# Modulation sums by transposes, narrower attention levels, and a low-rank column with its halves side by side: one decoder layer

## Chip, cores and metric

The kernel runs on one core of a Trainium2 chip. The metric is the device time of one execution in microseconds (us), the median of several runs. The core's engines run their own instruction queues in order: TensorE (PE, matrix multiplications and transposes, with its weight loads, PEld, beside them), VectorE (DVE), ScalarE (ACT), GpSimd (POOL) and SyncE (SP), from whose queue nearly all transfers (DMA) are issued.

## What is computed

One layer of a hybrid decoder, 256 tokens of width 2048, all in float32:

```python
mod = silu(c) @ w_ada + b_ada                      # six segments of 2048
shift1, scale1, gate1, shift2, scale2, gate2 = split(mod, 6)
h = rms_norm(x, norm1_gain) * (1 + scale1) + shift1
proj = h @ w_in                                    # 2048 x 13840, split into
#   stick-breaking q, k, v; dilated q, k, v; GLA q, k, v, r;
#   a_gla (16 columns, the low-rank forget gate); 3 x 2048 branch gates
a = a_gla @ w_gla_a + b_gla_a                      # 16 -> 512
log_a = log_sigmoid(a) / 16
o_gla = rms_norm(gla(q, k, v, log_a)) * silu(r)    # gated linear attention
y = g0 * (o_sb @ w_br_sb) + g1 * (o_dil @ w_br_dil) + g2 * (o_gla @ w_br_gla)
x = x + gate1 * (y @ w_out)
h = rms_norm(x, norm2_gain) * (1 + scale2) + shift2
x = x + gate2 * ((silu(gate) * up) @ w_ffn_out)    # gate, up = h @ w_ffn_in
```

In the gated linear attention the score of query i and key j (j not after i) is the sum over the channels of q_i k_j exp(cum_i - cum_j), where cum is the running sum of log_a over the tokens.

## The kernel before

**Matrix products.** Activations are kept transposed in 128-row chunks, split into a high part rounded to a reduced 32-bit matmul type (float32r) and a low part with the rest. Weights get the same split: `load_weights` (line 124) brings 1024 columns a partition (2 chunks of 512, or 8 chunks of 128) by one DMA into a buffer `raw`, ACT rounds it into `whi` (147), DVE subtracts into `wlo` (148). `raw`, `whi` and `wlo` are rings of four buffers each. `mm3` (lines 152 to 155) then makes three matmuls for each pair: high x high, high activation x low weight, low activation x high weight. `block` (157) runs them for one block of 512 output columns and both halves of the tokens into the four `acc` banks of PSUM; four further banks, `misc`, serve everything else. A matmul of plain float32 operands is also used (attention, sums, the low-rank gate).

**Modulation.** `ada_mac` (258) multiplies a row block of `w_ada` by one column of silu(c) and adds it to an accumulator `ada` on DVE, so that after 16 chunks the accumulator's sum over the 128 partitions is the wanted row. `column_sum` (301) makes that sum and turns the row into a column at once: the 128 x 128 piece of the accumulator is the stationary operand and a column of ones the moving one. `finish_columns` (303) adds the bias (307) and, for a scale, adds 1 and multiplies by the norm's gain (310). For the first norm the 16 chunks come in four groups (`GROUPS`, 3, 4, 4 and 5 chunks); `first_group` has its own code, `ada_group` (264) does the others in pieces of 4, 4, 2 and 3 chunks while `proj_block` already multiplies the preceding group with `w_in`. `h_group` then makes that group's part of h. For the second norm `columns` (798) does the same for 16 chunks of shift2 and of scale2 as a background generator, advanced by `tick` between matmuls; its result is used by `norm2` (line 1016).

**Mixing.** While the last group of chunks runs over the 13 blocks of `w_in`, `stick_breaking`, `gla` and `dilated` are placed among the matmuls. `gla` (618) first multiplies h with 128 columns of `w_in` that begin with the 16 of the low-rank gate: it loads them with `load_weights` and runs 16 x `mm3` with the weight stationary and 256 tokens moving, then copies 16 rows to `aT` and multiplies these with `w_gla_a`. The scores within a tile of 128 tokens are built by levels: for L = 1, 2, 4, ... 64, keys in the even runs of L tokens meet queries in the following odd run. Factors exp(...) for both sides lie in one tile `f`; `scatter` (674) multiplies the whole 128 x 128 tile for the 4 heads (678) and copies those entries that the level's 0/1 mask selects (679). Entries of level L have a key below 128 - L and a query from L on.

**Order.** The program's order is a proposal: a planner places the instructions on each engine by priorities (`prio` raises them) and by the buffers that are free; `issue_after` sets an instruction behind another one on its engine. Once placed, each engine's order is fixed.

Of the kernel before, what the change touches and what calls it, by code (L numbers as in the profile page):

```python
# [10 lines left out]
F32 = mybir.dt.float32  # L11
F32R = mybir.dt.float32r
# [25 lines left out]
GROUPS = ((0, 3), (3, 7), (7, 11), (11, 16))  # L38
GLA_LEVELS = (1, 2, 4, 8, 16, 32, 64)
NFF = 11  # L40
ROW_N1, ROW_N2, ROW_SBQ, ROW_SBK, ROW_DILQ, ROW_DILK, ROW_GB, ROW_GG = 16, 32, 48, 49, 50, 51, 52, 56


# [22 lines left out]
def trunk(ctx: ExitStack, tc: tile.TileContext, I, out):  # L66
# [11 lines left out]
    def nm(base):  # L78
        uid[0] += 1
        return f"{base}_{uid[0]}"  # L80

    def S(tag, shape, dtype=F32):
        return slot.tile(shape, dtype, tag=tag, name=nm(tag))

    def small(shape, dtype=F32, bufs=8):
        return sp.tile(shape, dtype, tag="tiny", name=nm("tiny"), bufs=bufs)

    def scr(shape, dtype=F32):
        return sp.tile(shape, dtype, tag="scr", name=nm("scr"))
# [4 lines left out]
    def misc_bank(shape):  # L94
        return psm.tile(shape, F32, tag="misc", name=nm("misc"))
# [28 lines left out]
    def load_weights(src, k0, k1, c0, w=NB, spare=(), ahead=True):  # L124

        parts = []
        step = (2 * NB) // w  # L130
        with prio() if ahead else nullcontext():
            for ka in range(k0, k1, step):
                n = min(step, k1 - ka)
                raw = wp.tile([P, step, w], F32, tag="raw", name=nm("raw"))
                nc.sync.dma_start(
                    raw[:, :n, :],
                    src[ka * P : (ka + n) * P, c0 : c0 + w].rearrange("(k p) c -> p k c", p=P),
                )
                i = len(spare) - (k1 - ka)
                if i >= 0:  # L140
                    hi = S(spare[i], [P, step, w], F32R)
                    lo = S(spare[i + 1], [P, step, w], F32R)
                else:
                    hi = wp.tile([P, step, w], F32R, tag="whi", name=nm("whi"), bufs=4)
                    lo = wp.tile([P, step, w], F32R, tag="wlo", name=nm("wlo"), bufs=4)
                with tc.issue_after(state["casts_after"]) if "casts_after" in state else nullcontext():
                    state["cast"] = nc.scalar.copy(hi[:, :n, :], raw[:, :n, :])  # L147
                state["split"] = nc.vector.tensor_tensor(lo[:, :n, :], raw[:, :n, :], hi[:, :n, :].bitcast(F32), op=ALU.subtract)  # L148
                parts += [(hi[:, i, :], lo[:, i, :]) for i in range(n)]
        return parts  # L150

    def mm3(ps, lh, ll, rh, rl, start, stop, seeded=False):
        nc.tensor.matmul(ps, lh, rh, start=start, stop=False, skip_group_check=seeded)  # L153
        nc.tensor.matmul(ps, lh, rl, start=False, stop=False, skip_group_check=seeded)  # L154
        state["mm"] = nc.tensor.matmul(ps, ll, rh, start=False, stop=stop, skip_group_check=seeded)  # L155
# [108 lines left out]
    def ada_group(k0, k1, tags=ADA_TAGS, between=None):  # L264

        n = k1 - k0
        sh, sc = mod1[:, 0, k0:k1], mod1[:, 1, k0:k1]
        count = 0
        pieces = -(-n // 4)
        for i in range(pieces):  # L270
            a = k0 + n * i // pieces
            m = k0 + n * (i + 1) // pieces - a
            w = m * P
            acc = S("ada", [P, 2, w])
            for k in range(KC):
                with prio():
                    raw = S(tags[count % len(tags)], [P, 2, w])
                    nc.sync.dma_start(
                        raw,
                        w_ada[k * P : (k + 1) * P, : 2 * D].rearrange("p (s c) -> p s c", s=2)[:, :, a * P : a * P + w],  # L280
                    )
                    ada_mac(acc, raw, k)
                count += 1
                if k < KC - 1:
                    yield
            if between is not None:
                between()
            with prio():
                o = a - k0
                for q in range(m):  # L290
                    ps = misc_bank([P, 2])
                    for j in range(2):
                        column_sum(ps[:, j : j + 1], acc[:, j, q * P : (q + 1) * P])
                    c = slice(o + q, o + q + 1)
                    finish_columns(ps[:, 0:1], sh[:, c], SEG_SHIFT1, a + q)
                    finish_columns(ps[:, 1:2], sc[:, c], SEG_SCALE1, a + q, ROW_N1)
            yield
        gains[GROUPS.index((k0, k1))] = (sh, sc)

    def column_sum(ps, acc):  # L300
        return nc.tensor.matmul(ps, acc, ones[:, 0:1], start=True, stop=True)  # L301

    def finish_columns(ps, dst, seg, k0, gain_row=None):

        n = dst.shape[1]
        o = seg * KC + k0
        nc.vector.tensor_tensor(dst, ps, bada[:, o : o + n], op=ALU.add)
        if gain_row is not None:
            g = vec[:, gain_row + k0 : gain_row + k0 + n]
            nc.vector.scalar_tensor_tensor(dst, dst, 1.0, g, op0=ALU.add, op1=ALU.mult)  # L310
# [229 lines left out]
    lvl_f = S("T4", [P, len(GLA_LEVELS) + 1, P])  # L540
    nc.sync.dma_start(lvl_f, I["k_lvl"])
    nc.gpsimd.tensor_copy(lvl, lvl_f)
    wga = kc[:16, 4:8, :].rearrange("p a b -> p (a b)")
    nc.sync.dma_start(wga, I["w_gla_a"])

    def head(c, t):
        return A[c // 4][:, t, (c % 4) * P : (c % 4 + 1) * P]
# [68 lines left out]


    def gla():
        aw = load_weights(w_in, 0, KC, COL_A, P)
        ps = misc_bank([P, T])  # L620
        for k in range(KC):
            hh = hT[0][k // 4][:, k % 4, :]
            hl = hT[1][k // 4][:, k % 4, :]
            mm3(ps, aw[k][0], aw[k][1], hh, hl, k == 0, k == KC - 1)
        aT = scr([16, T])
        nc.scalar.copy(aT, ps[:16, :])

        for b in (9, 10, 11, 12):
            proj_block(LAST, b)
# [41 lines left out]
        def at(x, h, t):  # L671
            return x[:, h * T + t * P : h * T + (t + 1) * P]

        def scatter(level, lhs, rhs):
            for t in range(NT):
                ps = misc_bank([P, N_GLA, P])
                for h in range(N_GLA):
                    nc.tensor.matmul(ps[:, h, :], at(lhs, h, t), at(rhs, h, t), start=True, stop=True)  # L678
                nc.vector.copy_predicated(
                    sc_same[t], lvl[:, level : level + 1, :].to_broadcast([P, N_GLA, P]), ps  # L680
                )

        scatter(len(GLA_LEVELS), kT, qT)
        for li, L in enumerate(GLA_LEVELS + (P,)):
            f = S(f"T{4 + li % 2}", [P, N_GLA * T])
            view = lambda x: x.rearrange("p (s two l) -> p s two l", two=2, l=L)
            fv, pw, sw, qw, kw = view(f), view(pre), view(suf), view(qT), view(kT)
            nc.scalar.activation(fv[:, :, 0, :], sw[:, :, 0, :], AF.Exp, scale=1.0 / 16.0)
            nc.scalar.activation(fv[:, :, 1, :], pw[:, :, 1, :], AF.Exp, scale=1.0 / 16.0)
            nc.vector.tensor_mul(fv[:, :, 0, :], fv[:, :, 0, :], kw[:, :, 0, :])  # L690
            nc.vector.tensor_mul(fv[:, :, 1, :], fv[:, :, 1, :], qw[:, :, 1, :])
            if L < P:
                scatter(li, f, f)
                ns = N_GLA * T // (2 * L)
                nc.vector.tensor_tensor(
                    sw[:, :, 0, :], sw[:, :, 0, :], pw[:, :, 1, L - 1 : L].to_broadcast([P, ns, L]), op=ALU.add
                )
                nc.vector.tensor_tensor(
                    pw[:, :, 1, :], pw[:, :, 1, :], pw[:, :, 0, L - 1 : L].to_broadcast([P, ns, L]), op=ALU.add
                )  # L700
            else:
                ps = misc_bank([P, N_GLA, P])
                for h in range(N_GLA):
                    nc.tensor.matmul(ps[:, h, :], at(f, h, 0), at(f, h, 1), start=True, stop=True)
                nc.scalar.copy(sc_cross, ps)
# [92 lines left out]
    def columns(seg, acc):  # L798
        for _ in range(4):
            yield  # L800
        v = const.tile([P, KC], F32, name=nm("mod2"))
        for i in range(0, KC, 4):
            ps = misc_bank([P, 4])
            for j in range(4):
                with tc.issue_after(state["mm"].ins):
                    column_sum(ps[:, j : j + 1], acc[:, (i + j) * P : (i + j + 1) * P])
                if j % 2:
                    yield
            finish_columns(ps, v[:, i : i + 4], seg, i, ROW_N2 if seg == SEG_SCALE2 else None)
        mod2[seg] = v  # L810

    def rows_of(name, seg, acc):
# [344 lines left out]
```

## Time and profile before

| what | us |
|---|---|
| median of 3 runs | 1636.75 (1636.34 to 1638.01) |
| profiled execution | 1638.33 |
| its span | 1636.6 |
| casts on ACT (line 147, 1024 wide), busy | 549.4 |
| subtractions on DVE (line 148, 1024 wide), busy | 636.6 |
| low-rank column on PE, first to last start | 338.5 to 344.2 |
| levels on PE, first to last start | 364.4 to 401.3 |
| core's granted TensorE clock | 1.00 |

A row of a group in this profile reads: line, engine, operation, output <- inputs with their shapes, count | busy us, mean ns of one | idle time of the engine just before them, and what ended it. A row of the timeline begins with the start and the duration. A row of the waits gives who waited for whom, then us in total, times, and the longest. Matmuls of one engine overlap: the next begins before the last one's result is written, so a mean duration is longer than the distance from start to start.

### The profile page before, as it was taken

The page shows a single profiled execution, that of the slowest core. Times are in us where ns is not written, and L with a number is a line of the kernel's source. Part 1 is how long each engine was busy: PE and PEld are TensorE (multiplying, and loading weights), DVE is VectorE, ACT ScalarE, POOL GpSimd, SP SyncE. Part 2 cuts the span into 40 slices and gives each one's busy share as a digit, 9 for nine tenths or more (in the row PEclk, how much of TensorE's full clock was granted, in tenths as well). Part 3 has the DMA queues.
Part 4 walks back from the last instruction along what each step waited for, and adds up shares of the span by engine and source line. Part 5 has one row for each costly group of instructions (what it writes and reads, how often), then busy time and mean ns, then how long its engine had stood idle before and what let it go on. Part 6 is the DMA issues. An engine that isn't in the chain of part 4 may idle for free.

```text
span 1636.6 us, 20156 instructions
## 1 busy us (share of the span) xinstructions
PE 1617.2 (99%) x7420; PEld 1333.7 (81%) x7420; DVE 1120.2 (68%) x1342; ACT 798.2 (49%) x1126; POOL 5.9 (0%) x14
## 2 busy tenths in 40 slices
PE   8999999999999999999999999999999999999998
PEld 7888888778778888788887888888888888888887
DVE  6789996879688687877756566767655555454453
ACT  5654449764765444444445644444444444433332
POOL 1000000000000000000000000000000000000000
PEclk9999999999999999999999999999999999999999
DMA  9999986876778889888756478887766666666663
GB/s 318 340 324 320 331 283 209 257 229 186 224 233 276 289 303 320 294 272 310 260 185 222 133 229 268 274 262 257 220 187 191 182 191 189 190 206 193 206 206 110
DMA packets 194563, 395.93 MB, mean 242 GB/s; under 512 B 12899, under 2 KB 27913, under 8 KB 194465
## 3 DMA queue, kind: packets, MB, share of 16 engines
q1 hardware_dynamic: 194240, 394.63, 74.3%
q8 instruction: 58, 0.95, 0.2%
q14 instruction: 41, 0.33, 0.1%
q0 software_dynamic: 224, 0.01, 0.0%
HBM read 392.50 MB, written 2.10 MB: 241 GB/s over the span
## 4 chain that ended last, share of the span: by engine, by line
PE 90%; DMA 4%; DVE 3%; ACT 2%; issue 1%; SPq 0%; DVEq 0%; ACTq 0%
PE acc L154 28%; PE acc L155 28%; PE acc L153 28%; DMA raw<-w_in 2%; DVE wlo L148 1%; DMA A<-w_ada 1%; PE misc L678 1%; ACT whi L147 1%; PE misc L943 1%; PE misc L301 1%; DVE ada L258 1%; DMA raw<-w_br_gla 0%; PE misc L572 0%; DMA AR<-w_ada 0%; DMA raw<-w_ffn_in 0%
## 5 line engine op out<-in xcount | busy, mean ns | idle before, releaser
L148 DVE TENSOR_TENSOR wlo<-raw,whi 128x1024 fp32r<-128x1024 f32 (+1 forms) x548 | 653.6, 1197 | 436.4 <-ACT whi L147 432.9
L147 ACT CAST whi<-raw 128x1024 fp32r<-128x1024 f32 (+1 forms) x548 | 564.7, 1033 | 720.0 <-PE acc L155 559.0
L154 PE MATMUL acc<-wlo,H 128*128 128x512 f32 x1576 | 617.0, 391 | 4.8 <-DVE wlo L148 4.5
L155 PE MATMUL acc<-whi,H 128*128 128x512 f32 x1576 | 615.3, 391 | 0.0
L153 PE MATMUL acc<-whi,H 128*128 128x512 f32 x1576 | 614.6, 392 | 0.6 <-ACT H L408 0.5
L154 PEld LDWEIGHTS acc<-wlo,H 128*128 128x128 f32 x1576 | 296.0, 188 | 68.9 <-DVE wlo L148 9.5
L155 PEld LDWEIGHTS acc<-whi,H 128*128 128x128 f32 x1576 | 295.9, 188 | 61.8 <-DVE H L1021 0.9
L153 PEld LDWEIGHTS acc<-whi,H 128*128 128x128 f32 x1576 | 295.6, 188 | 61.5 <-ACT H L408 0.9
L153 PE MATMUL acc<-whi,A 128*128 128x512 f32 x312 | 122.4, 392 | 0.0
L154 PE MATMUL acc<-wlo,A 128*128 128x512 f32 x312 | 121.5, 390 | 0.8 <-DVE wlo L148 0.8
L155 PE MATMUL acc<-whi,A 128*128 128x512 f32 x280 | 109.1, 390 | 0.0
L258 DVE SCALAR_TENSOR_TENSOR ada<-AR,csil,ada 128x1024 f32<-128x1024 f32 x59 | 75.1, 1279 | 3.2 <-DMA AR<-w_ada 3.1
L154 PEld LDWEIGHTS acc<-wlo,A 128*128 128x128 f32 x312 | 58.6, 188 | 12.9 <-DVE wlo L148 1.1
L153 PEld LDWEIGHTS acc<-whi,A 128*128 128x128 f32 x312 | 58.6, 188 | 12.2 <-ACT whi L147 0.3
L155 PEld LDWEIGHTS acc<-whi,A 128*128 128x128 f32 x280 | 52.5, 188 | 11.1
L153 PE MATMUL acc<-whi,T 128*128 128x512 f32 x120 | 46.8, 390 | 0.0
L155 PE MATMUL acc<-whi,T 128*128 128x512 f32 x120 | 46.7, 389 | 0.0
L154 PE MATMUL acc<-wlo,T 128*128 128x512 f32 x120 | 46.7, 389 | 0.0
L155 PE MATMUL acc<-whi,OS 128*128 128x512 f32 x112 | 43.6, 389 | 0.0
L258 DVE SCALAR_TENSOR_TENSOR ada<-OS,csil,ada 128x1024 f32<-128x1024 f32 (+2 forms) x33 | 35.5, 1075 | 0.8 <-DMA OS<-w_ada 0.5
L453 DVE TENSOR_TENSOR A<-A,acc 128x512 f32<-128x512 f32 x48 | 31.9, 684 | 5.1 <-PE acc L155 4.9
L451 ACT COPY A<-acc 128x512 f32<-128x512 f32 x50 | 28.4, 585 | 11.8 <-PE acc L155 10.8
(327 smaller groups left out, 1246.1 us busy)
## 6 DMA issues: line engine op xcount, KB each, us to landing
raw<-w_in SPq DMA_DIRECT2D x205, 512.0 KB, 4.8
raw<-w_ffn_in SPq DMA_DIRECT2D x176, 512.0 KB, 3.8
raw<-w_ffn_out SPq DMA_DIRECT2D x88, 512.0 KB, 4.7
AR<-w_ada SPq DMA_DIRECT2D x79, 512.0 KB, 4.7
raw<-w_out SPq DMA_DIRECT2D x32, 512.0 KB, 3.9
KC<-w_ada SPq DMA_DIRECT2D x30, 512.0 KB, 5.2
KD<-w_ada SPq DMA_DIRECT2D x19, 512.0 KB, 5.5
OS<-w_ada SPq DMA_DIRECT2D x16, 512.0 KB, 7.3
```

The source lines that it names most:

```text
L147: state["cast"] = nc.scalar.copy(hi[:, :n, :], raw[:, :n, :])
L148: state["split"] = nc.vector.tensor_tensor(lo[:, :n, :], raw[:, :n, :], hi[:, :n, :].bitcast(F32), op=ALU.subtract)
L153: nc.tensor.matmul(ps, lh, rh, start=start, stop=False, skip_group_check=seeded)
L154: nc.tensor.matmul(ps, lh, rl, start=False, stop=False, skip_group_check=seeded)
L155: state["mm"] = nc.tensor.matmul(ps, ll, rh, start=False, stop=stop, skip_group_check=seeded)
L258: nc.vector.scalar_tensor_tensor(acc, raw, c, acc, op0=ALU.mult, op1=ALU.add)
L301: return nc.tensor.matmul(ps, acc, ones[:, 0:1], start=True, stop=True)
L451: nc.scalar.copy(A[b][:, t, :], pss[t])
L453: nc.vector.tensor_add(A[b][:, t, :], A[b][:, t, :], pss[t])
L678: nc.tensor.matmul(ps[:, h, :], at(lhs, h, t), at(rhs, h, t), start=True, stop=True)
L943: nc.tensor.transpose(ps[:, i, :], src[:, i * P : (i + 1) * P], ident)
```

## The change

Four edits. The sum over partitions is made by transposing the 128 x 128 pieces (up to four into one bank) and adding along the rows on DVE; in `columns` the bias and gain are applied once at the end, on all 16 columns. `scatter` gets the level's L and uses keys 0 to 127 - L and queries L to 127 alone. The 16 low-rank columns are split into a tile `T6` of their own, high and low side by side as 32 stationary columns: one matmul with the high part of h gives both products (rows 0 to 15 and 16 to 31), a second one adds the low part of h times the high weights to rows 0 to 15. `w_gla_a` is loaded twice, below itself, so that the product with the 32 rows adds the halves. `first_group` and `rows_of` stay as they are.

```diff
--- before.py
+++ after.py
@@ -38,6 +38,7 @@
 GROUPS = ((0, 3), (3, 7), (7, 11), (11, 16))
 GLA_LEVELS = (1, 2, 4, 8, 16, 32, 64)
 NFF = 11
+RANK = 16
 ROW_N1, ROW_N2, ROW_SBQ, ROW_SBK, ROW_DILQ, ROW_DILK, ROW_GB, ROW_GG = 16, 32, 48, 49, 50, 51, 52, 56
 
 
@@ -286,19 +287,26 @@
             if between is not None:
                 between()
             with prio():
-                o = a - k0
-                for q in range(m):
-                    ps = misc_bank([P, 2])
-                    for j in range(2):
-                        column_sum(ps[:, j : j + 1], acc[:, j, q * P : (q + 1) * P])
-                    c = slice(o + q, o + q + 1)
-                    finish_columns(ps[:, 0:1], sh[:, c], SEG_SHIFT1, a + q)
-                    finish_columns(ps[:, 1:2], sc[:, c], SEG_SCALE1, a + q, ROW_N1)
+                c = slice(a - k0, a - k0 + m)
+                sums = small([P, 2, m])
+                for j in range(2):
+                    turned_sums(sums[:, j, :], acc[:, j, :])
+                finish_columns(sums[:, 0, :], sh[:, c], SEG_SHIFT1, a)
+                finish_columns(sums[:, 1, :], sc[:, c], SEG_SCALE1, a, ROW_N1)
             yield
         gains[GROUPS.index((k0, k1))] = (sh, sc)
 
     def column_sum(ps, acc):
         return nc.tensor.matmul(ps, acc, ones[:, 0:1], start=True, stop=True)
+
+    def turned_sums(dst, acc, behind=None):
+
+        n = dst.shape[1]
+        ps = misc_bank([P, n, P])
+        for i in range(n):
+            with tc.issue_after(behind) if behind is not None else nullcontext():
+                nc.tensor.transpose(ps[:, i, :], acc[:, i * P : (i + 1) * P], ident)
+        nc.vector.reduce_sum(dst, ps, axis=AX.X)
 
     def finish_columns(ps, dst, seg, k0, gain_row=None):
 
@@ -540,8 +548,9 @@
     lvl_f = S("T4", [P, len(GLA_LEVELS) + 1, P])
     nc.sync.dma_start(lvl_f, I["k_lvl"])
     nc.gpsimd.tensor_copy(lvl, lvl_f)
-    wga = kc[:16, 4:8, :].rearrange("p a b -> p (a b)")
-    nc.sync.dma_start(wga, I["w_gla_a"])
+    wga = kc[: 2 * RANK, 4:8, :].rearrange("p a b -> p (a b)")
+    for i in range(2):
+        nc.sync.dma_start(wga[i * RANK : (i + 1) * RANK, :], I["w_gla_a"])
 
     def head(c, t):
         return A[c // 4][:, t, (c % 4) * P : (c % 4 + 1) * P]
@@ -616,14 +625,26 @@
 
 
     def gla():
-        aw = load_weights(w_in, 0, KC, COL_A, P)
+
+        hl = S("T6", [P, KC, 2, RANK], F32R)
+        for k in range(0, KC, 8):
+            raw = wp.tile([P, 8, P], F32, tag="raw", name=nm("raw"))
+            with prio():
+                nc.sync.dma_start(raw, w_in[k * P : (k + 8) * P, COL_A : COL_A + P].rearrange("(k p) c -> p k c", p=P))
+                hi, lo = hl[:, k : k + 8, 0, :], hl[:, k : k + 8, 1, :]
+                nc.scalar.copy(hi, raw[:, :, :RANK])
+                nc.vector.tensor_tensor(lo, raw[:, :, :RANK], hi.bitcast(F32), op=ALU.subtract)
         ps = misc_bank([P, T])
         for k in range(KC):
-            hh = hT[0][k // 4][:, k % 4, :]
-            hl = hT[1][k // 4][:, k % 4, :]
-            mm3(ps, aw[k][0], aw[k][1], hh, hl, k == 0, k == KC - 1)
-        aT = scr([16, T])
-        nc.scalar.copy(aT, ps[:16, :])
+            nc.tensor.matmul(
+                ps[: 2 * RANK], hl[:, k].rearrange("p a r -> p (a r)"), hT[0][k // 4][:, k % 4, :],
+                start=k == 0, stop=k == KC - 1, skip_group_check=True,
+            )
+            nc.tensor.matmul(
+                ps[:RANK], hl[:, k, 0, :], hT[1][k // 4][:, k % 4, :], start=False, stop=k == KC - 1, skip_group_check=True
+            )
+        aT = scr([2 * RANK, T])
+        nc.scalar.copy(aT, ps[: 2 * RANK, :])
 
         for b in (9, 10, 11, 12):
             proj_block(LAST, b)
@@ -671,13 +692,15 @@
         def at(x, h, t):
             return x[:, h * T + t * P : h * T + (t + 1) * P]
 
-        def scatter(level, lhs, rhs):
+        def scatter(level, lhs, rhs, L=0):
+
+            n = P - L
             for t in range(NT):
                 ps = misc_bank([P, N_GLA, P])
                 for h in range(N_GLA):
-                    nc.tensor.matmul(ps[:, h, :], at(lhs, h, t), at(rhs, h, t), start=True, stop=True)
+                    nc.tensor.matmul(ps[:n, h, L:], at(lhs, h, t)[:, :n], at(rhs, h, t)[:, L:], start=True, stop=True)
                 nc.vector.copy_predicated(
-                    sc_same[t], lvl[:, level : level + 1, :].to_broadcast([P, N_GLA, P]), ps
+                    sc_same[t][:n, :, L:], lvl[:n, level : level + 1, L:].to_broadcast([n, N_GLA, n]), ps[:n, :, L:]
                 )
 
         scatter(len(GLA_LEVELS), kT, qT)
@@ -690,7 +713,7 @@
             nc.vector.tensor_mul(fv[:, :, 0, :], fv[:, :, 0, :], kw[:, :, 0, :])
             nc.vector.tensor_mul(fv[:, :, 1, :], fv[:, :, 1, :], qw[:, :, 1, :])
             if L < P:
-                scatter(li, f, f)
+                scatter(li, f, f, L)
                 ns = N_GLA * T // (2 * L)
                 nc.vector.tensor_tensor(
                     sw[:, :, 0, :], sw[:, :, 0, :], pw[:, :, 1, L - 1 : L].to_broadcast([P, ns, L]), op=ALU.add
@@ -800,13 +823,9 @@
             yield
         v = const.tile([P, KC], F32, name=nm("mod2"))
         for i in range(0, KC, 4):
-            ps = misc_bank([P, 4])
-            for j in range(4):
-                with tc.issue_after(state["mm"].ins):
-                    column_sum(ps[:, j : j + 1], acc[:, (i + j) * P : (i + j + 1) * P])
-                if j % 2:
-                    yield
-            finish_columns(ps, v[:, i : i + 4], seg, i, ROW_N2 if seg == SEG_SCALE2 else None)
+            turned_sums(v[:, i : i + 4], acc[:, i * P : (i + 4) * P], state["mm"].ins)
+            yield
+        finish_columns(v, v, seg, 0, ROW_N2 if seg == SEG_SCALE2 else None)
         mod2[seg] = v
 
     def rows_of(name, seg, acc):
```

## Prediction

> **What bounds the kernel now.** I read the page first, then TensorE's groups by shape, its timeline around the places the change touches, the waits from 262 to 350 us, and VectorE's groups.
>
> ```profile
> PE 1617.2 (99%) x7420; PEld 1333.7 (81%) x7420; DVE 1120.2 (68%) x1342; ACT 798.2 (49%) x1126; POOL 5.9 (0%) x14
> PE 90%; DMA 4%; DVE 3%; ACT 2%; issue 1%; SPq 0%; DVEq 0%; ACTq 0%
> ```
>
> TensorE (PE) is busy in 99% of the span and carries 90% of the chain that ended last. So an instruction taken from PE shortens the kernel by its cadence (the time from its start to the next start), unless PE then has to wait for somebody. PE's idle time is 1636.6 - 1617.2 = 19.4 us. The groups by shape for what is changed (first size stationary, second moving):
>
> ```profile
> L301 PE MATMUL misc<-ones,ada 128*128 128x1 f32 x128 | 15.4, 238 | 0.0
> L678 PE MATMUL misc<-T 128*128 128x128 f32 x112 | 13.8, 276 | 0.0
> L943 PE MATMUL misc<-ident,scr 128*128 128x128 f32 x88 | 11.4, 272 | 0.0
> L591 PE MATMUL misc<-A,A 128*128 128x256 f32 x12 | 3.6, 386 | 0.0
> L153 PE MATMUL misc<-H,whi 128*128 128x256 f32 x16 | 4.6, 288 | 0.0
> ```
>
> There are 64 column sums (6 in the first group, 26 for the later groups, 32 in `columns`), but x128: a plain f32 matmul is two instructions. Line 943 makes 11 x 2 x 4 = 88 transposes and counts x88: a transpose is one. The means (238 to 288 ns) are latencies; these instructions overlap, so I price by starts in the timeline:
>
> ```profile
> 152.30 1.93 PE L301 MATMUL misc<-ones,ada 128*128 128x1 f32 x16
> ...
> 154.09 0.48 PE L154 MATMUL acc<-wlo,H 128*128 128x512 f32 x1
> ...
> 338.52 0.36 PE L153 MATMUL misc<-H,whi 128*128 128x256 f32 x1
> ...
> 344.35 0.40 PE L155 MATMUL acc<-whi,H 128*128 128x512 f32 x1
> ...
> 950.23 1.03 PE L943 MATMUL misc<-ident,scr 128*128 128x128 f32 x8
> 951.02 0.48 PE L153 MATMUL acc<-whi,H 128*128 128x512 f32 x1
> ```
>
> 16 column-sum instructions hold PE for 154.09 - 152.30 = 1.79 us (0.11 each), 8 transposes for 0.79 us (0.10 each), and the 48 matmuls of the low-rank column for 344.35 - 338.52 = 5.83 us (inside the run they start 0.1195 us apart). PE's one long wait near the change:
>
> ```profile
> PE acc L154 <- DVE wlo L148: 3.8, 2, 2.9
> ACT whi L147 <- PE acc L155: 6.4, 11, 1.3
> ACT whi L147 <- PE misc L154: 4.2, 2, 2.4
> ```
>
> The last row says that two casts of weights (at 341.6 and 344.4 us) waited for the low-rank column's own matmuls. The reader should see why: `gla` loads that column with `load_weights`, which takes two of the four `whi` and two of the four `wlo` buffers. Between 264 and 279 us the cast row has four 1024-wide casts before the one 512-wide cast where every block of this stage needs two and one; the extra two are that column's. It is consumed only from 338.5 us, so for some 65 us the blocks run on half a ring, and eleven casts wait for PE to free one. It ends in this:
>
> ```profile
> 329.50 1.05 ACT L147 CAST whi<-raw 128x1024 fp32r<-128x1024 f32 x1 [0.25 <-PE acc L155]
> 331.75 1.28 DVE L258 SCALAR_TENSOR_TENSOR ada<-AR,csil,ada 128x1024 f32<-128x1024 f32 x1 [1.91 <-DMA AR<-w_ada]
> 332.95 1.22 DVE L148 TENSOR_TENSOR wlo<-raw,whi 128x1024 fp32r<-128x1024 f32 x1
> 334.22 0.50 PE L154 MATMUL acc<-wlo,H 128*128 128x512 f32 x1 [2.88 <-DVE wlo L148]
> ```
>
> The cast comes late for want of a buffer, its subtraction stands behind a multiply-add that waits for a DMA, and PE stands 2.88 us.
>
> **The change part by part.** (1) *Sums.* 58 sums (26 + 32) become transposes; the first group's 6 stay. The 52 instructions of the later groups hold PE for 1.70, 1.79, 0.81 and 1.26 us (bursts at 84.5, 152.3, 191.2, 233.9) = 5.6 us. The 64 in `columns` come mostly in fours of 0.36 us: 16 x 0.36 = 5.8 us. After it, 26 transposes at 0.10 us = 2.6 us and 32 in fours of 0.36 us (line 912's fours: 512.42 to 512.77) = 2.9 us. Gain 11.4 - 5.5 = 5.9 us.
>
> VectorE (DVE) takes up what PE gives back:
>
> ```profile
> L751 DVE TENSOR_REDUCE dmax<-T 128x1 f32<-128x256 f32 x6 | 2.5, 410 | 0.0
> L751 DVE TENSOR_REDUCE dmax<-T 128x1 f32<-128x128 f32 x6 | 1.7, 280 | 0.0
> L307 DVE TENSOR_TENSOR mod<-misc,bada 128x1 f32<-128x1 f32 x32 | 3.6, 153 | 2.3 <-PE misc L301 2.2
> ```
>
> A reduction costs 0.28 us for 128 and 0.41 for 256 elements, so about 0.54 for 384 and 0.67 for 512. The groups' four pieces (4, 4, 2, 3 chunks) need two each: 2 x (0.67 + 0.67 + 0.41 + 0.54) = 4.6 us, against 39 small operations of 0.15 us that become 12: -4.1. `columns` gains 8 x 0.67 = 5.4 us and drops 12 small operations for 3: -1.4. The column's two casts and subtractions shrink from 8 x 128 to 8 x 16 elements a partition: two subtractions of 1.22 us become about 0.29 each (line 600's 128-wide row): -1.9. With up to 1 us off the predicated copies, DVE's sum rises by under 2 us of 1120; DVE is off the path on average. Where it is on it is a group's end: at 84.5 to 86.7 us the small operations trail the sums by 0.5 us and the next subtraction starts right behind them (86.70), for which PE waits 0.38 us. There PE would arrive some 0.9 us earlier, while two reductions of 0.67 us and three small operations end no earlier than now. At 152, 191 and 234 us PE has other matmuls ready. Cost between 0 and 0.9 x 4 = 3.6 us; I take 0.5, the 84 us place in part. In `columns` no one waits for the result until line 1016 at 897 us, so finishing all 16 columns at the end costs nothing; cover gone, it would be one operation of 0.16 us.
>
> (2) *Low-rank column.* 48 matmuls become 32, moving width unchanged at 256. No row has a stationary tile of 16 or 32 columns. If the cadence stays 0.1195 us, 16 fewer save 1.9 us; if it falls to half of the 512-wide matmul's 0.2275 us, 5.74 - 32 x 0.114 = 2.1. I take 2.0. The loads of the column are the same two of 512 KB. The second copy of `w_gla_a` is one more SP issue (0.46 us, the first is at 252.49); SP's next issue is at 255.36, so it hides in that gap, and it would delay one weight load by 0.46 us without it.
>
> (3) *The ring.* With the column in `T6` the four `whi` and `wlo` buffers all serve the blocks. Worth at least 0 (DVE's order may keep the multiply-add and its late DMA ahead of the subtraction) and at most PE's two waits in that table, 3.8 us, and the 0.4 us that its weight loads wait for ACT's casts there, 4.2 us. I take the long one, 2.9: with two spare buffers the cast would be a block's third ahead, some 3 us, about what the wait is long.
>
> (4) *Levels.* 112 instructions in bursts of 16 that hold PE about 1.78 us (111 ns each), 12.5 us. A f32 instruction goes by its moving columns: 256 take 0.215 us (326.79 to 327.22 for two), 384 take 0.325 (334.79 to 335.44). Moving 128 - L columns leaves 769 of 896, so up to 14% of 12.5 = 1.8 us. But line 301 moves one column and still takes 0.09 to 0.11 us, which reads as a floor set by loading 128 stationary columns; were that fixed, the gain is 112 x 0.006 = 0.7 us or less. The stationary side is cut to 128 - L as well. I take 1.3, between the two; below nothing is a rival.
>
> The Trainium skill ("TensorE: Matmul & The Clock Gate", LDWEIGHTS) says that a weight load takes time in proportion to its columns, not its rows. By that rule the floor shrinks with the moving side and the whole 1.8 us would come, a sum 0.5 us lower; no run here has loaded fewer than 128 columns.
>
> Sum: -5.9 + 0.5 - 2.0 - 2.9 - 1.3 = **-11.6 us**. The profiled execution has a span of 1636.6 and took 1638.33; the median of the runs is 1636.75. Span 1636.6 - 11.6 = 1625.0, median 1636.75 - 11.6 = **1625.2**.
>
> **Rivals.** A difference of 0.2% (3.3 us) is about what a measurement of this kernel tells from no change: 1633.5 to 1640.
>
> (a) *The long wait stays.* Its cause is partly DVE waiting for a DMA (1.91 us), and a freed buffer does not oblige the planner to use it earlier. For: DVE executes in order. Against: in this stage nearly every cast waits for a buffer. Then 1636.75 - 8.7 = 1628.1.
>
> (b) *The reductions stand in the way.* Each holds DVE 0.67 us at a stretch where now operations of 0.15 us let subtractions through; PE's waits for `wlo` say this engine can stop it. All 16 passed on whole: 4.6 + 5.4 = 10.0 us against 8.7 gained (less the 0.5 counted already): 1637.6, no change. Against: a burst of 16 sums costs DVE the same time now.
>
> (c) *Slower: narrow stationary tiles lose the hidden load.* Today a load (191 ns by its row) runs behind the matmul before it. If a partial tile stops that, the 112 level and 32 column instructions pay up to 0.19 us each: 27 us, 1652.6. It decides from 11.6 / 144 = 0.08 us each. For: no such row here. Against: line 638's 16-row tile (8 in 345.83 to 347.75, 0.24 us for 256 columns) is 0.025 us over line 591's 0.215, no more.
>
> (d) *A new order, slower.* The planner places everything anew; the move of one DMA-bound multiply-add cost 2.9 us at 334. More than five such new waits (15 us) make it 1640 and more, say 1641.
>
> (e) *A transpose is two instructions after all* for this tile: the sums gain nothing, 1625.2 + 5.9 = 1631.1. Against: line 943's count.
>
> (f) *The clock.* Granted clock is 1.00 in every stretch I asked for, those with 16 transposes in a row (272.25 to 273.91) among them. If each of 12 new bursts halved it over the ten 512-wide matmuls behind (2.3 us), 12 x 2.3 = 28 us: 1653. The Trainium skill (the same page, Part 4: PE-mode transpose) holds that transposes do not count as activity for the clock; by its rule such a loss could come, and the rows above do not bear it out.
>
> **How the numbers follow.** Forecast 0.52, (a) 0.25, (b) 0.11, (c) 0.05, (d) 0.04, (e) 0.02, (f) 0.01. Faster: forecast, (a), (e) = 0.79; same: (b) = 0.11; slower: (c), (d), (f) = 0.10. The forecast's own range is 1620 (5.9 + 2.1 + 4.2 + 1.8 = 14.0 with no stall gives 1622.7, and some freed waits elsewhere) to 1629; with (a) and (e) and a part of (b) it reaches 1635.
>
> **What would show it.** Line 301 down to x12, 58 transposes in its place; PE at 7420 - 116 + 58 - 16 = 7346 instructions. The column's run about 3.8 us instead of 5.8. No cast waiting for the misc matmuls of `gla`, and no PE wait of 2 us or more between 300 and 345 us. Level bursts falling from about 1.78 us to some 0.9 to 1.0 at L = 64. Reductions near 0.67 us, and the matmuls behind the group ends waiting no more than 1 us. I am wrong if level bursts do not shrink or grow, if PE's idle time rises by more than 3 us over 19.4, or if DVE's reductions head a new row of PE waits.

## The result, and the profile after

| | before | after |
|---|---|---|
| median, us | 1636.55 (1635.34 to 1638.01) | 1628.80 (1627.64 to 1630.80) |
| ratio | 1 | 0.9948 [0.9936, 0.9961] |
| span of the profiled execution, us | 1636.6 | 1629.0 |
| PE idle in it, us | 19.4 | 20.9 |
| table loads on ACT | 8 | 12 |

The changed kernel is 7.75 us faster (6.4 to 10.5 by the interval of the ratio); 11.6 were forecast. The terms of the sum can be found in the profile near their forecast sizes. What is missing was lost elsewhere, most of it some 100 us behind the low-rank column. The first lines of the page and of the chain of waits:

```profile
PE 1608.1 (99%) x7346; PEld 1325.8 (81%) x7346; DVE 1121.9 (69%) x1322; ACT 801.5 (49%) x1130; POOL 5.3 (0%) x14
PE 88%; DMA 5%; DVE 3%; ACT 2%; issue 1%; SPq 0%; DVEq 0%; ACTq 0%
```

PE executes the 7346 instructions counted ahead, and DVE is 1.7 us busier, as forecast (under 2). PE is busy 9.1 us less, its idle time is 1.5 us longer. The groups by shape:

```profile
L308 PE MATMUL misc<-ident,ada 128*128 128x128 f32 x58 | 8.3, 273 | 0.0
L309 DVE TENSOR_REDUCE mod<-misc 128x4 f32<-128x512 f32 x8 | 5.3, 681 | 0.7 <-PE misc L308 0.7
L639 PE MATMUL misc<-H,T 128*32 128x256 f32 x16 | 3.8, 282 | 0.0
L643 PE MATMUL misc<-H,T 128*16 128x256 f32 x16 | 3.7, 276 | 0.0
```

The 58 sums are 58 transposes, one instruction each. A reduction of 512 elements takes 0.68 us (0.67 forecast). The low-rank column has 16 + 16 matmuls with 32 and 16 stationary columns. The means are still latencies; what an edit is worth stands in the starts, here in PE's timeline:

```profile
84.78 1.03 PE L308 MATMUL misc<-ident,ada 128*128 128x128 f32 x8
85.58 0.48 PE L154 MATMUL acc<-whi,H 128*128 128x512 f32 x1
...
347.08 0.36 PE L639 MATMUL misc<-H,T 128*32 128x256 f32 x1
...
350.81 0.40 PE L156 MATMUL acc<-whi,H 128*128 128x512 f32 x1
...
398.52 1.15 PE L701 MATMUL misc<-T 128*64 128x64 f32 x16
399.60 0.50 PE L156 MATMUL acc<-whi,H 128*128 128x512 f32 x1
```

Eight transposes hold PE 85.58 - 84.78 = 0.80 us, the column 350.81 - 347.08 = 3.73 us (5.83 before), and the level L = 64 takes 399.60 - 398.52 = 1.08 us for 16 instructions. Against that, the waits of PE by who ended them, first in the kernel before, then in the changed one:

```profile
PE acc L154 <- DVE wlo L148: 5.3, 5, 2.9
...
PE misc L787 <- DVE T L783: 2.1, 1, 2.1
...
PE misc L572 <- DVE A L565: 0.3, 1, 0.3
```

```profile
PE misc L581 <- DVE A L574: 2.7, 1, 2.7
...
PE misc L810 <- DVE T L806: 1.7, 1, 1.7
PE acc L155 <- DVE wlo L149: 1.6, 2, 1.0
...
PE misc L581 <- ACT A L582: 0.9, 1, 0.9
```

The waits for `wlo` (lines 154 and 148 before, 155 and 149 now) fall from 5.3 to 1.6 us; the 2.88-us one at 334 us is gone, and so are the casts that waited for the low-rank column's matmuls. But the transposes of the dilated branch's norms (line 581) now stand 2.7 us behind DVE, where this line (572 before) waited 0.3 us. The other wait at line 581, 0.9 us behind ACT, is not at this place: the same helper makes the norms of `stick_breaking`, and there it stands, at 274 us:

```profile
274.31 1.23 PE L581 MATMUL misc<-ident,A 128*128 128x128 f32 x8 [0.86 <-ACT A L582]
```

The way back from the 2.7 us, on ACT's timeline:

```profile
445.06 1.28 ACT L914 ACT_TABLE_LOAD   x1
446.35 1.06 ACT L914 ACTIVATE A<-A 128x1024 f32<-128x1024 f32 x1
...
448.37 1.28 ACT L242 ACT_TABLE_LOAD   x1
449.66 0.21 ACT L242 ACTIVATE tiny<-tiny 128x8 f32<-128x8 f32 x1
...
450.83 1.28 ACT L243 ACT_TABLE_LOAD   x1
...
454.48 1.28 ACT L242 ACT_TABLE_LOAD   x1
...
456.00 1.28 ACT L243 ACT_TABLE_LOAD   x1
```

Line 914 is the sigmoid of a branch gate, a loop that the change does not touch. Its gate was copied by 439.75 us (903) and its result is first read behind 579 us (977), so the planner may put it wherever ACT looks free. In the new order it stands between the squares (569) and the logarithm (242) of a norm in `dilated`. It loads its function table; then the Ln loads one, the Exp (243) another, and the next norm's Ln and Exp load theirs again. These are 5 loads of 1.28 us, 6.4 us of ACT time, and casts of weights stand between them. The scaling of the first of these two norms (574) then comes late on DVE, also because DVE's order has the second norm's first step (245), a multiply-add and a subtraction ahead of it; its factors had been ready at 455.95 us:

```profile
457.53 0.16 DVE L245 TENSOR_TENSOR tiny<-tiny 128x4 f32<-128x4 f32 x1 [1.58 <-ACT tiny L243]
457.61 1.28 DVE L259 SCALAR_TENSOR_TENSOR ada<-AR,csil,ada 128x1024 f32<-128x1024 f32 x1
458.81 1.22 DVE L149 TENSOR_TENSOR wlo<-raw,whi 128x1024 fp32r<-128x1024 f32 x1
459.94 0.68 DVE L574 TENSOR_TENSOR A<-A,tiny 128x512 f32<-128x512 f32 x1
```

PE's next transposes stand still meanwhile. In the order of before, the first of these sigmoids loads its table right behind the last norm's Exp, and the norms load nothing:

```profile
450.75 0.21 ACT L242 ACTIVATE tiny<-tiny 128x4 f32<-128x4 f32 x1
450.98 1.28 ACT L895 ACT_TABLE_LOAD   x1
```

The wait has an aftermath. First PE's timeline, then its windows (stretch, length, busy us of PE, PEld, DVE, ACT and POOL with the number of instructions, granted clock, DMA share, GB/s):

```profile
460.68 0.66 PE L581 MATMUL misc<-ident,A 128*128 128x128 f32 x4 [2.66 <-DVE A L574]
...
462.38 0.63 PE L155 MATMUL acc<-wlo,H 128*128 128x512 f32 x1
462.81 0.63 PE L156 MATMUL acc<-whi,H 128*128 128x512 f32 x1
```

```profile
455.00:460.00 5.00, 3.02 (x14) 2.17 (x12) 3.42 (x6) 4.34 (x6) 0.00 (x0) 1.00 0.76 225
460.00:465.00 5.00, 4.32 (x17) 3.56 (x18) 4.21 (x10) 1.53 (x2) 0.00 (x0) 0.68 0.89 289
465.00:470.00 5.00, 5.00 (x33) 4.55 (x31) 4.25 (x15) 2.78 (x9) 0.00 (x0) 0.98 0.72 229
```

Behind the wait 512-wide matmuls start 0.43 us apart instead of 0.2275: the granted clock is 0.68 in this stretch, which costs 5 x 0.32 = 1.6 us. Together: 2.66 of wait, less the 0.3 of before, + 1.6 = 4.0 us. The same profile has one more slow stretch early on, which the profile of before lacks (1.00 there); it costs 5 x 0.34 = 1.7 us:

```profile
35.00:40.00 5.00, 5.00 (x16) 3.94 (x16) 4.89 (x10) 2.27 (x4) 0.00 (x0) 0.66 0.79 291
```

### The profile page after: what moved, and what is told of

Read it like the earlier page. It is cut to its first block, busy times and chain, and to the rows that moved or that the text cites. A ratio compares the mean times of both kernels' runs of the same rounds, so it can differ in the third digit from the quotient of the medians.

```text
span 1629.0 us, 19997 instructions
## 1 busy us (share of the span) xinstructions
PE 1608.1 (99%) x7346; PEld 1325.8 (81%) x7346; DVE 1121.9 (69%) x1322; ACT 801.5 (49%) x1130; POOL 5.3 (0%) x14
## 4 chain that ended last, share of the span: by engine, by line
PE 88%; DMA 5%; DVE 3%; ACT 2%; issue 1%; SPq 0%; DVEq 0%; ACTq 0%
PE acc L156 28%; PE acc L154 28%; PE acc L155 27%; DMA raw<-w_in 2%; DMA raw<-w_br_gla 1%; ACT whi L148 1%; DMA A<-w_ada 1%; DVE wlo L149 1%; DMA KD<-w_ada 1%; PE misc L701 1%; PE misc L962 1%; DVE ada L259 1%; PE misc L308 0%; DMA raw<-w_ffn_in 0%; PE misc L613 0%
## 5 line engine op out<-in xcount | busy, mean ns | idle before, releaser
L154 PEld LDWEIGHTS acc<-whi,A 128*128 128x128 f32 x312 | 58.6, 188 | 11.9
```

## The experiments

Two theories had to be told apart. **N**: the terms hold, and the new order with that sigmoid between Ln and Exp takes some 4 to 5 us back. **The rival**: the terms themselves are smaller than worked out, or overlap, and the place at 445 to 465 us only shows slack that would have appeared elsewhere. Each run is compared with the kernel before on its own chip, so ratios are compared, not bare medians.

### The sigmoids pinned behind dilated's last Exp

The three sigmoids of the gates, as below, and the two of line 917 in the same way, may not be issued before the last Exp of `dilated`; nothing else is edited. The same edit was made in the kernel before.

```diff
-        nc.scalar.activation(lse, lse, AF.Exp)
+        state["last_exp"] = nc.scalar.activation(lse, lse, AF.Exp)
...
     for br in range(3):
-        nc.scalar.activation(gates[0, br], gates[0, br], AF.Sigmoid)
+        with tc.issue_after(state["last_exp"].ins):
+            nc.scalar.activation(gates[0, br], gates[0, br], AF.Sigmoid)
```

> The changed kernel, with the five sigmoids behind the first gate blocks set behind the last Exp of the dilated branch on ScalarE. Theory N (the terms came as predicted, but the planner's new order puts a sigmoid at 446 us between the Ln and Exp of the dilated norms, whose table loads delay them until TensorE waits 2.7 + 0.9 us at line 581 and then runs at half clock for some 3.5 us): no table loads at lines 242 and 243, no wait at 581, about 5 us less than the changed kernel, 1623 to 1625 us. Rival S (the terms were too large, the wait at 581 only shows slack that would be lost at another place): 1628 to 1630 us.

> The kernel before with the same pin. It tells whether the pin is worth anything without the change. Theory N: before has its sigmoids placed so that only the softmax of the dilated branch reloads tables (lines 753, 758, 766), and TensorE waits 2.1 us at line 787; within 2.5 us of before, 1634 to 1637 us. Rival S, and any theory by which the pin is simply a better kernel: some 4 to 5 us faster than before, 1632 us.

The changed kernel pinned: 1624.83 us, ratio 0.9920 [0.9909, 0.9932]. The kernel before pinned: 1634.70, ratio 0.9982 [0.9973, 0.9991]. The Ln and Exp of the same norm on ACT's timeline of the pinned changed kernel, and the window behind them:

```profile
445.94 0.21 ACT L242 ACTIVATE tiny<-tiny 128x8 f32<-128x8 f32 x1 [0.49 <-DVE tiny L240]
...
447.20 0.20 ACT L243 ACTIVATE tiny<-tiny 128x8 f32<-128x8 f32 x1
```

```profile
460.00:465.00 5.00, 5.00 (x24) 4.14 (x23) 4.98 (x16) 4.57 (x14) 0.00 (x0) 1.00 0.28 82
```

No table load stands ahead of either; in the whole kernel 4 loads are left of 12. PE is busy throughout this window at clock 1.00, and of the waits at line 581 only 0.2 us is left, at the early norms. (The 0.9 us that the expectation adds to the 2.7 belongs to the early norms too, not to this place.) This is N's number. That the pin is worth 3.0 us on the kernel before too was not foreseen; it is more than the 2.5 that N allowed and less than the rival's 4 to 5. PE's wait of 2.1 us at line 787 (`dilated`'s products) disappears, and its waits for `wlo` shrink from 5.3 to

```profile
PE acc L154 <- DVE wlo L148: 3.9, 5, 1.4
```

(this is the pinned kernel before, its waits of PE). So the two pinned kernels are to be set against each other: 0.9920 / 0.9982 = 0.9938, or 10.2 us of 1637 (with the half widths 0.0012 and 0.0009 added in squares, about 7.7 to 12.6). That is what the change is worth when the sigmoids' place is taken out of the comparison.

### The same again, on one chip, and the table loads put back

The gap between the changed kernel and its pinned form was measured again, with a third kernel beside them. That one is pinned, but has one extra small sigmoid (128 x 8, its result unused) ahead of the Ln of `dilated`'s third norm:

```diff
-    def rsqrt(ss, inv_n, shape):
+    def rsqrt(ss, inv_n, shape, sig=False):
...
+        first = nc.scalar.activation(small(shape), v, AF.Sigmoid) if sig else None
+        with tc.issue_after(first.ins) if sig else nullcontext():
+            nc.scalar.activation(y, v, AF.Ln)
...
-        qk_norm(6, 0, 4, kn)
+        qk_norm(6, 0, 4, kn, sig=True)
```

> The changed kernel beside its pinned form on one chip: ratio 0.995 to before.

> The pinned form on the same chip as the changed kernel: ratio 0.992 to before, 4 to 6 us under the changed kernel; if the first measurement was luck of the chip, within 2 us of it.

> The changed kernel with the pin, and one small extra sigmoid (128 x 8, its result unused) on ScalarE right before the Ln of the third dilated norm, which is where the changed kernel's planner had put a sigmoid. Theory N (that place costs the changed kernel its 5 us): five more table loads (one for the sigmoid, two at line 242, two at line 243), a TensorE wait of 2 us or more at the norm's transposes, a drop of the clock behind it, and 3 to 5 us more than the pinned kernel: 1628 to 1630. Rival (the loads are hidden, the pin helped by something else): 1624 to 1626 and no such wait.

| kernel | median, us | ratio to before |
|---|---|---|
| changed | 1630.10 | 0.9950 [0.9937, 0.9964] |
| changed, pinned | 1623.26 | 0.9915 [0.9902, 0.9929] |
| changed, pinned, one extra sigmoid | 1626.94 | 0.9937 [0.9924, 0.9949] |

The pin is worth 1630.10 - 1623.26 = 6.8 us here, more than the 4 to 6 expected, and the intervals lie apart. It moves all five sigmoids, and the two profiles show that it clears two places. In the changed kernel PE waits 2.7 us at line 581, 1.6 at 810 and 1.0 at 813 (both `dilated`'s products), in the pinned one 0.8 at 810 alone; the slow clock behind 460 us (0.66 in 5 us) costs 1.7. That is 5.3 - 0.8 + 1.7 = 6.2 us, of which the norms have 2.7 + 1.7 = 4.4.

The extra sigmoid gives 3.7 of the 6.8 back, between what the two theories said. The intervals of these two ratios just overlap, but the slowest run of the pinned kernel (1624.38) is no slower than the fastest of this one (1624.39). ACT's timeline with it:

```profile
443.49 1.28 ACT L242 ACT_TABLE_LOAD   x1
...
445.95 1.28 ACT L244 ACT_TABLE_LOAD   x1
...
448.41 1.28 ACT L245 ACT_TABLE_LOAD   x1
...
453.50 1.28 ACT L244 ACT_TABLE_LOAD   x1
...
455.01 1.28 ACT L245 ACT_TABLE_LOAD   x1
```

The five loads are back (242 is the sigmoid here, 244 and 245 are Ln and Exp), 1.0 to 2.4 us earlier. Two more come with them, at the softmax's Ln and Exp (474.09 and 476.76 us), where the pinned kernel has none. PE's wait behind the five is shorter:

```profile
PE misc L583 <- DVE A L576: 1.1, 1, 1.1
```

and the clock stays at 1.00 from 450 to 465 us. So one misplaced sigmoid, by its loads, is enough to cost time. How the 3.7 us come about is not shown in full: this profile is of the fastest of the five executions, 2.55 us below their median, and has 1.1 us at the norms and 0.6 more than the pinned one at the products. The longer wait and the drop of the clock belong to the planner's own order, in which a sigmoid of 1.06 us and casts stand among the loads as well and DVE scales the first norm behind the second one's step; this remaining part (about 3 us) was not reproduced piece by piece.

### The ring alone

In the kernel before, the column's four split weights are sent into spare tiles `T0` to `T3`, so that the rings' buffers stay with the blocks; the 48 matmuls stay.

```diff
-        aw = load_weights(w_in, 0, KC, COL_A, P)
+        aw = load_weights(w_in, 0, KC, COL_A, P, spare=("T0", "T1") + (None,) * 6 + ("T2", "T3") + (None,) * 6)
```

> The kernel before, in which the low-rank column's split weights lie in the tiles T0 to T3 in place of two whi and two wlo buffers. Same casts, same matmuls. Theory R (the column starved the ring): no cast waits for the column's matmuls, TensorE's waits for wlo between 262 and 350 us fall from 3.8 us to under 1, and the time by 2.9 us to 1633.8. Rival (the wait is the DMA behind the multiply-add): that wait stays, 1636 to 1637 us.

1634.61 us, 0.9981 [0.9972, 0.9989]: 3.1 us faster, near the forecast's 2.9. Two rows of its waits of PE:

```profile
PE misc L572 <- ACT A L573: 2.1, 1, 2.1
...
PE acc L154 <- DVE wlo L148: 0.7, 3, 0.4
```

The waits for `wlo` fall from 5.3 to 0.7 us, so the held ring was what made them. A new wait of 2.1 us takes a part back, at the transposes of the early norms:

```profile
278.34 0.66 PE L572 MATMUL misc<-ident,A 128*128 128x128 f32 x4 [2.10 <-ACT A L573]
```

No table load is near it; ACT has casts and copies to do before it empties these transposes' bank (573). This order also has loads ahead of an Ln and an Exp of `dilated` (455.59 and 458.05 us), and PE does not wait behind them. So an edit that touches none of these lines dealt the order anew here too, but the loss is of another kind, and loads at the norms do not cost in every order.

### Each part alone

The sums alone are the hunks of `ada_group`, `turned_sums` and `columns`, the column alone those of `RANK`, `w_gla_a` and `gla`, the levels alone those of `scatter`. The core of each, in this order:

```diff
-                    column_sum(ps[:, j : j + 1], acc[:, (i + j) * P : (i + j + 1) * P])
+            turned_sums(v[:, i : i + 4], acc[:, i * P : (i + 4) * P], state["mm"].ins)
...
-            mm3(ps, aw[k][0], aw[k][1], hh, hl, k == 0, k == KC - 1)
+                ps[: 2 * RANK], hl[:, k].rearrange("p a r -> p (a r)"), hT[0][k // 4][:, k % 4, :],
...
-                scatter(li, f, f)
+                scatter(li, f, f, L)
```

> The kernel before with the transposed sums alone. By the predicted term 5.9 us less TensorE time, 0.5 us given back at the group's end: 1631 us. If the reductions stand in the way, 1635 to 1638, with TensorE waiting for wlo behind line 309's reductions.

> The kernel before with the low-rank column side by side alone (the copy of w_gla_a below itself included). Predicted terms: 2.0 us of TensorE time and 2.9 us of the ring's wait, 4.9 us. TensorE busy 1615.1; no cast waits for the column's matmuls and the wait for wlo at 334 us is gone. If a new order puts a sigmoid between the dilated branch's Ln and Exp, table loads at lines 241 and 242 show it and 2 to 4 us are given back.

> The kernel before with the narrower levels alone. The bursts of the changed kernel add up to 1.5 us less TensorE time; with the order otherwise unchanged 1.5 us faster, which is inside the interval of the measurement. More than 3 us either way would be the order, not the levels, and would have to show in TensorE's waits.

> The changed kernel once more, beside the parts. As the sum of parts it would be 5.4 (sums as predicted) to 8.2 (as measured alone) + 4.9 + 1.5 = 12 to 15 us faster. If the new order costs it what the pin gave back, 8 to 9 us faster (ratio 0.995), with the wait at line 581 in every profile.

| kernel | median, us | ratio to before | PE busy against before, us |
|---|---|---|---|
| sums alone | 1630.20 | 0.9950 [0.9939, 0.9962] | -6.2 |
| column alone | 1633.36 | 0.9970 [0.9960, 0.9979] | -3.0 |
| levels alone | 1635.73 | 0.9994 [0.9985, 1.0003] | -2.3 |
| all (the changed kernel) | 1630.29 | 0.9955 [0.9942, 0.9967] | -8.7 |

By ratio the three are worth 8.2, 4.9 and 1.0 us, 14.1 together; the whole is worth 7.4. So the sums and the column hold by themselves, and the three do not add. The levels' own gain lies within its interval of nothing. The column alone has its own accident, first in the waits of PE, then in the windows:

```profile
PE misc L801 <- DVE T L797: 3.3, 1, 3.3
```

```profile
500.00:505.00 5.00, 4.56 (x20) 4.00 (x21) 4.04 (x14) 1.15 (x3) 0.00 (x0) 0.66 0.94 361
```

Line 801 is `dilated`'s products, where the kernel before waited 2.1 us (line 787). A table load (488.23 us) and a sigmoid with another load (496.24) stand on ACT ahead of it, and the clock falls behind the wait as it did at 460 us in the changed kernel. The sums alone have the like at the same products: a wait of 1.99 us up to 483.91 us, and a clock of 0.66 from 485 to 490.

### Two parts with the sigmoids pinned

The edits above and the pin together.

> The low-rank column alone with the sigmoids pinned behind the last Exp of the dilated branch. Against before with the pin (3.0 us faster than before) it should show the column's two terms alone: 3.0 + 4.9 = 7.9 us faster than before, less what the pin and the ring take from the same waits (up to 1.4 us of wlo waits), so 6.5 to 8.

> The sums alone with the pin. By the parts 8.2 (sums alone) + 3.0 (pin alone) = 11 us faster than before if both stand by themselves; 8 to 9 if what the sums gained over their term of 5.4 was the same waits in the dilated branch that the pin takes away.

Column and pin: 1631.24, 0.9965 [0.9952, 0.9979]. Sums and pin: 1627.40, 0.9940 [0.9928, 0.9953]. Both gain less than the pin's 3.0 and the part's own gain together, 5.7 of 7.9 and 9.8 of 11.2 us, but within their intervals of some 2 us to either side. The 5.7 lies below the 6.5 to 8 expected; the 9.8 lies between the two values named, and decides for neither. That the pin and the column partly remove the same waits (line 787/801, and those for `wlo`) would fit, and is not shown. Against the pinned kernel before (0.9982) the sums are worth 0.9958, or 6.9 us, and the column 0.9983, or 2.8. With the levels' 1.0, which were not run pinned, this makes 10.7, against 10.2 for the whole change in pinned form. In a steadied order the parts do add, as far as intervals of about 2 us to either side can tell.

The fastest kernel of the case is the changed one with the pin: 1624.83 and 1623.26 in its two measurements, 0.9920 and 0.9915 of the kernel before.

## Why the prediction was right, and where it was not

It forecast 1625.2 us, in a range of 1620 to 1635, and the time was 1628.8. That is 0.2 us inside the forecast's own part of the range (1620 to 1629) and 0.7 us from the number of rival (a), 1628.1, whose long wait did not stay. So the time alone could not have told the two apart, and that it fell in this part is partly luck. The terms against the starts in the trace of the changed kernel:

| term | forecast | measured | from |
|---|---|---|---|
| sums | -5.9 | -5.5 | group bursts 5.56 to 2.52 us, `columns` about 5.8 to 3.3 |
| group ends | +0.5 | +1.0 | waits at 88 us: 0.38 before, 1.00 and 0.40 after |
| low-rank column | -2.0 | -2.1 | 5.83 to 3.73 us |
| ring | -2.9 | -3.8 | waits for `wlo` between 262 and 355 us, 3.8 to none |
| levels | -1.3 | -1.5 | seven bursts, 12.09 to 10.62 us |
| sum | -11.6 | -11.9 | |

**The step that failed** is none of these. It is the silent one in their sum, that the rest of the order stays as it was. Rival (d), a new planner order, named the mechanism and even the reason ("the planner places everything anew"). But it was priced only as a rout, more than five new waits and 15 us, and so was given 0.04. What came was chiefly one place: 4.0 us by the trace. -11.9 + 4.0 = -7.9, against -7.6 in the span. That the two agree so well is luck: the same profile has 0.9 us of new wait at 274 us and 1.7 us of slow clock at 35 us, and with these the account stands at -5.3, so more than 2 us of gain have no entry in it. With the sigmoids pinned in both kernels the change is worth 10.2 us (7.7 to 12.6), and the forecast sum of 11.6 lies inside; the parts fit less well there (sums 6.9 where 5.4 were forecast, column with ring 2.8 where 4.9 were). A term for the order, plus or minus 3 us around the sum, would have been the honest form: the pin alone moved the kernel before by 3.0 us, and the changed one by 6.8.

**Sums.** They held, and by the run alone even more came (8.2 us): beside 6.2 us of PE's busy time the waits for `wlo` fell by 1.9. *Rival (b)*, the reductions in the way (its 1637.6 leaves out the ring's 2.9 without saying why), falls with it: no reduction heads a wait of PE, and only the group end at 88 us is worse, by 1.0 us. It is of the kind forecast, twice the size. *Rivals (e) and (f)* fall too: 58 transposes are 58 instructions, and the clock drops behind waits, not behind transposes.

**Low-rank column.** Its cadence fell to 0.114 us, half a 512-wide matmul's, the lower of the two cadences weighed.

**The ring.** Both waits went, not the long one alone, so the 2.9 was short by 0.9. The size is that of one order, though: with the ring still held, the wait near 334 us is 1.14 us in the kernel before with the pin and 1.25 with the levels alone. *Rival (a)* falls: the freed buffers were used earlier, though nothing obliged the planner to. Alone the edit brought 3.1 us, after giving some back at line 572.

**Levels.** *Rival (c)*, narrow stationary tiles that lose the hidden load, falls: the bursts of 16 shrink from 1.69 us at 127 columns to 1.08 at 64. That is 0.106 and 0.0675 us an instruction, a slope of 0.6 ns a column above a fixed 0.03 us. So the floor does shrink with the tile, but not all of the 1.8 us comes. The rows of the weight loads show it too; their means are latencies, and fall by some 0.87 ns a column above a fixed 80:

```profile
L701 PEld LDWEIGHTS misc<-T 128*127 128x127 f32 x16 | 1.9, 190 | 0.1
...
L643 PEld LDWEIGHTS misc<-H,T 128*16 128x16 f32 x16 | 1.5, 94 | 0.1
...
L701 PEld LDWEIGHTS misc<-T 128*64 128x64 f32 x16 | 1.0, 138 | 0.4 <-issue 0.4
```

The Trainium skill ("TensorE: Matmul & The Clock Gate", LDWEIGHTS) has the load's time go by its columns; the direction agrees, while in strict proportion 64 columns would take 0.053 us.

**What stays open.** PE's busy time in the parts alone fell by 6.2 + 3.0 + 2.3 = 11.5 us, where the starts of the three edits account for 9.1; where the other 2.4 us lie was not followed. The gap is rather larger, for the profiles of the sums (0.69 from 35 to 40 us, 0.66 from 485 to 490) and of the column (0.66 from 500 to 505) hold some 5 us of slow clock that the one of before lacks. Why the planner put the sigmoid at that place was not tried either: a kernel cannot show what a planner would have weighed.

## What to carry to other kernels

When a planner places the work, each edit deals the whole order anew, and a sum of local terms is good only to the worth of one unlucky place, here 3 to 7 us. Look for work that is ready early and wanted late (a gate's sigmoid), and tie it behind the stage that it could disturb: it was the cheapest gain of the case, with or without the change. And a small operand that is fetched long ahead of its use should not sit in the buffers that the main stream turns over.

## What was not expected of the hardware

**Tables.** Once a sigmoid's table is in, an Ln and the next Exp each load one, 1.28 us a load, and two norms in a row load four; with the sigmoid gone none does. The Trainium skill ("ScalarE: Activation LUTs", Table sets: the hidden batching unit) has ln and then exp as one load from a shared set. The trace of the changed kernel differs: there each of the two has a load of its own. Which sets these loads name, it does not show.

**The clock after a wait.** PE waits of 2.66 us (up to 460.68 us in the changed kernel), 3.34 us (up to 500.44, the column alone) and 1.99 us (up to 483.91, the sums alone) were followed by a granted clock of 0.68, 0.66 and 0.66 over 5 us. But the kernel before waited 2.88 us at 334 us and 2.14 us at 487 us, the second at the same products as the 1.99, and kept 1.00. Length alone does not decide it. In windows of 1 us the clock of the changed kernel is 0.50 from 462 to 465 us. The Trainium skill ("TensorE: Matmul & The Clock Gate", Part 1: The HAM clock gate) tells of half rate after an idle window of about 3.4 us on a window that runs freely. Half rate agrees with the 0.50; but waits of 1.99 and 2.66 us, shorter than that figure, came ahead of it here.

A second stretch of the same kind, 0.66 between 35 and 40 us, stands in the profiles of the changed kernel's first and third measurement and not in its second one, at a place that no edit touches and behind a wait of only 0.44 us in the first. So a few microseconds of a single profile can be chance of this sort, and only medians tell them.
